# Differential attention heads turned to tokens and back by VectorE in 32 x 32 squares and DRAM, in place of TensorE transposes

## The chip, the cores and the metric

The kernel runs on one core of a Trainium2 chip, in one launch. The metric is the device time of an execution in microseconds. A core has TensorE (PE, with its weight loads PEld), VectorE (DVE), ScalarE (ACT), GpSimd (POOL) and SyncE (SP, which here issues transfers). PE writes to PSUM, in banks of 128 x 512 float32; the other tiles lie in SBUF, 128 partitions wide. Each engine works through its own queue in order; semaphores tie the queues together.

## The reference

One layer of a streaming encoder on 512 tokens of width 1024. A norm of x feeds four parallel mixers: A differential attention, B forgetting attention, C a convolution module, D a short gated convolution. Each is projected to the model width, gated, summed and projected out; then come cross-attention and a gated MLP. The change lies in mixer A, behind its attention:

```python
ya = _diff_attention(a_q..., a_k..., a_v..., lam, t_pos)      # (B, S, 4 heads, 128)
ya = (_rms_norm(ya, diff_norm[l]) * (1.0 - lambda_init)).reshape(B, S, BR_W)
...
proj = jnp.einsum('bsnc,ncd->bsnd', br, w_branch[l])          # br stacks ya, yf, yc, ys
```

For each token and head the 128 channels are divided by their root mean square, then scaled by a gain per channel.

## The kernel before, in words

**Tiling.** Activations are channel-major: channels on the partitions, the 512 tokens along the free axis. Every float32 operand is split into a high and a low part (`split`, lines 152 to 159: ACT writes the high part, DVE the low one), and each product is three matmuls (`mm3`). A block of weights of 512 KB is loaded by SP into a raw tile (`wr`, two buffers, line 176), cast by ACT to `wh` (line 190) and split by DVE to `wl` (line 191), four buffers each. `run_blocks` fetches the weights of three jobs ahead and then runs the job's body.

**A head.** `a_task(h)` does head h: in steps 0 to 3 scores of one block of 128 queries (two halves, PSUM tag `sc`), softmax on DVE and ACT, and the difference of the two (line 853); in steps 1 to 4 the probabilities of the step before are transposed on PE (tag `tr`) and split; in steps 3 and 5 `values` multiplies them with v into a bank of tag `av` (two buffers). At the end of step 5 ACT copies the bank to SBUF (line 858), channel-major, 128 channels by 512 tokens. Then the norm, lines 861 to 878: four PE transposes turn the head to tokens in a `tr` bank; ACT squares it (864), DVE sums over channels (866), POOL makes the reciprocal root (`rstd_of`, 268 and 271), DVE multiplies (868); four more PE transposes turn it back, and `split` with the gain as its scale writes `y["a"]` (tag `y8b`), which branch A's projection reads.

**What sets the order.** Three things. The jobs come in the order of `mixer_jobs`: for h = 0 to 3 the q and k projections of head h, each followed by 0, 2, 4 or 6 jobs of branch C's gate and projection; then `bg.drain("a")`, then the values of the forgetting attention (`vf_jobs`), its q and k, and between those branch A's gate and projection. The heads are background tasks (class `Background`): generators that yield a cost and a wait. A clock counts PE work (0.00042 a column of a matmul, 0.107 a transpose); at each tick, after every job and in the middle of a long one, the first two tasks of the queue may step, if credit (0.7 of the clock, at most 4) is left and the task's wait has passed. So `yield cost, 3.5` means: not again before the clock is 3.5 further. `drain` steps all tasks of a name to the end, waits or no waits. Last, the framework gives every instruction its place in the engines' queues, from this order and from its own estimate of when operands and buffers are ready.

**Buffers that matter.** In `vf_jobs` the first two token blocks take two banks of tag `mm` and two of tag `av`; the result goes to a tile of tag `v`, of which there is one, held by the heads' values (`va`) until the last head is done. Tags `ck` and `fbias` (two buffers each, 128 x 512) belong to `f_task`: rows of the cumulated log-forget and the score bias.

**A turn that is there already.** `conv_norm_task` (lines 670 to 709) turns the convolution's 512 x 512 result to tokens and back: four `V.transpose` (32 x 32 squares within a tile), four stores from SP to a DRAM tile (line 680), four loads (line 683).

Of the kernel before, what the change touches and what calls it, by code (L numbers as in the profile page):

```python
# [17 lines left out]
F32 = mybir.dt.float32  # L18
F32R = mybir.dt.float32r
AF = mybir.ActivationFunctionType  # L20
ALU = mybir.AluOpType
AX = mybir.AxisListType
# [3 lines left out]
P = 128  # L26
S = 512
# [56 lines left out]
def hybrid_layer(ctx: ExitStack, tc: tile.TileContext, a: dict, out: bass.AP):  # L84
# [12 lines left out]
    def bank(tag=None):  # L97
        if tag is None:
            turn_of.n += 1
            tag = "av" if turn_of.shared and turn_of.n % 2 else "mm"  # L100
        return psum.tile([P, 512], F32, tag=tag, name=f"ps_{tag}", bufs=2)
# [133 lines left out]
    def transpose(ps, x, n=P):  # L235
        PE.transpose(ps, x, ident[:n, :n])  # L236
        bg.clock += 0.107
# [75 lines left out]
    def e4(dtype=F32):  # L313
        return m1p.tile([P, 2, S], dtype, tag="e", name="e", bufs=3)
# [108 lines left out]
    def turn(t, half):  # L423
        ps = turned[t, half] = bank("av" if half else "tr")
        for k in range(4):
            keep(PE.transpose(ps[:, k * P:(k + 1) * P], y01[t][:, (half * 4 + k) * P:(half * 4 + k + 1) * P], ident))
# [229 lines left out]
    def conv_task(j):  # L656
# [5 lines left out]
        for k in range(n - 1):  # L662
# [4 lines left out]
                conv_ends.append(ins.ins)  # L667
            yield 0.66, 0.0

    def conv_norm_task():  # L670
        xn = m1p.tile([P, 5, S], F32, tag="qk", name="xn", bufs=2)
        tok, chan = (dram.tile([S, S], F32, name=n) for n in ("conv_tok", "conv_chan"))

        def turn(rows, squares, src):
            for i in range(4):
                V.transpose(squares[:, i], src[:, i])
                yield 0.65, 0.0
            form = rows.rearrange("(b r) (j a c) -> a r j b c", r=32, a=4, c=32)
            for a in range(4):
                SP.dma_start(form[a], squares[a * 32:a * 32 + 32].rearrange("r j (b c) -> r j b c", c=32))  # L680
            yield 0.0, 4.0
            for i in range(4):
                SP.dma_start(xn[:, i], rows[i * P:(i + 1) * P, :])
            yield 0.0, 5.0

        yield 0.0, 2.0
        while len(conv_ends) < 4:
            yield 0.0, 0.5
        yield from turn(tok, conv_u, conv_y)
        for t in range(NT):  # L690
            st = m1p.tile([P, 6], F32, tag="bn6", name="bn6", bufs=2)
            mv = m1p.tile([P, 2], F32, tag="bn2", name="bn2", bufs=2)
            V.bn_stats(st, xn[:, t])
            V.bn_aggr(mv, st)
            r = rstd_of(m1p, [mv[:, 1:2]])
            V.tensor_scalar(xn[:, t], xn[:, t], mv[:, 0:1], r, ALU.subtract, ALU.mult)
            yield 1.5, 0.0
        yield from turn(chan, conv_y, xn)
        while "d" in y:
            yield 0.0, 2.0  # L700
        yield 0.0, 2.0
        y["c"] = (y8(), y8())
        for j in range(4):
            e = e4()
            A.activation(e[:, 0], xn[:, j], AF.Identity, bias=pc("ln_b", j), scale=pc("ln_g", j))
            A.activation(e[:, 1], xn[:, j], AF.Tanh, bias=half["ln_b"][:, j:j + 1], scale=half["ln_g"][:, j:j + 1])
            V.scalar_tensor_tensor(e[:, 0], e[:, 1], 1.0, e[:, 0], ALU.add, ALU.mult)
            split(e[:, 0], y["c"][0][:, j], y["c"][1][:, j], 0.5)
            yield 1.4, 1.0
# [109 lines left out]
                m1p.tile([P, 4, 256], F32R, tag="ptl", name="ptl", bufs=2))  # L819


    def a_task(h, qk, v):
        es, pt, av = {}, None, None
        for step in range(6):
            if step in (3, 5):
                if av is None:
                    av = bank("av")
                vh, vl = (x[:, :, h * P:(h + 1) * P] for x in v[0])
                values(av, lambda kt: ((vh[:, kt], 0), (vh[:, kt], 1), (vl[:, kt], 0)), pt, step // 2 - 1)
            cost = 0.0  # L830
            if 1 <= step <= 4:
                if step in (1, 3):
                    pt = pt_tiles()
                to_keys_major(es.pop(step - 1)[:, 0], step, pt[0], pt[1], (step - 1) % 2)
                cost += 0.1 + 0.15 * step
            if step < 4:
                qt, w = step, (step + 1) * P
                e = es[qt] = e4()
                st = m1p.tile([P, 8], F32, tag="st8", name="st8", bufs=4)
                for c in range(2):  # L840
                    ps = bank("sc")
                    scores(ps, qk, c, qt * P, w)
                    V.tensor_tensor_reduce(e[:, c, :w], ps[:, :w], mask_a[:, S - w:], scale=1.0,
                                           scalar=-3.0e38, op0=ALU.add, op1=ALU.max,
                                           accum_out=st[:, c:c + 1])
                V.tensor_scalar(st[:, 2:4], st[:, 0:2], -HD ** -0.5, None, ALU.mult)
                for c in range(2):
                    A.activation(e[:, c, :w], e[:, c, :w], AF.Exp, bias=st[:, 2 + c:3 + c],
                                 scale=HD ** -0.5, accum_out=st[:, 4 + c:5 + c])
                V.reciprocal(st[:, 6:8], st[:, 4:6])  # L850
                V.tensor_scalar(st[:, 7:8], st[:, 7:8], lam, None, ALU.mult)
                A.activation(e[:, 1, :w], e[:, 1, :w], AF.Copy, scale=st[:, 7:8])
                V.scalar_tensor_tensor(e[:, 0, :w], e[:, 0, :w], st[:, 6:7], e[:, 1, :w], ALU.mult,
                                       ALU.subtract)
                cost += 0.6 + 0.0035 * w
            if step == 5:
                e = e4()
                A.copy(e[:, 0], av)
            yield cost, 3.5

        ps = bank("tr")
        for t in range(NT):
            transpose(ps[:, t * P:(t + 1) * P], e[:, 0, t * P:(t + 1) * P])
        A.activation(e[:, 1], ps, AF.Square, scale=1.0 / math.sqrt(P))
        ms = m1p.tile([P, NT], F32, tag="ms4", name="ms4", bufs=2)
        V.tensor_reduce(ms, e[:, 1].rearrange("p (t c) -> p t c", t=NT), AX.X, ALU.add)
        r = rstd_of(m1p, [ms], NT)
        V.tensor_tensor(e[:, 0].rearrange("p (t c) -> p t c", t=NT),
                        ps.rearrange("p (t c) -> p t c", t=NT),
                        r.unsqueeze(2).to_broadcast([P, NT, P]), ALU.mult)  # L870
        yield 1.5, 3.5
        ps2 = bank("tr")
        for t in range(NT):
            transpose(ps2[:, t * P:(t + 1) * P], e[:, 0, t * P:(t + 1) * P])
        if "a" not in y:
            y["a"] = (y8b(), y8b())
        split(ps2, y["a"][0][:, h], y["a"][1][:, h], half["dn"])
        yield 0.6, 0.0


# [874 lines left out]
```

## Time and profile before

| | us |
|---|---|
| median of 3 runs | 1061.96 (1061.37 to 1063.41) |
| the profiled execution | 1061.46 |
| its span, first to last instruction | 1059.7 |
| PE busy in the span | 1048.7 |

In rows of instructions the columns are start, duration, engine, line, operation, output and inputs, shapes and count; a value in brackets is the idle time ahead and what ended it. Grouped rows give the busy time (overlapping instructions counted once) and the mean ns of one. The view of one source line gives minimum, median and maximum ns, first and last start, and below it what the engine waited for ahead of these instructions, or who waited for them, as microseconds and times. Rows of waits read: who, for whom, total, times, longest. In the rows of windows stand the busy time and count of PE, PEld, DVE, ACT and POOL, PE's granted clock, the DMA share and GB/s.

### The profile page before, as it was taken

Reading aid. Unit: us, or ns where it says so; the run is one execution under the profiler, and the core shown is the slowest. Engines: PE = TensorE matmul, PEld = TensorE weight load, DVE = VectorE, ACT = ScalarE, POOL = GpSimd, SP = SyncE. Lnnn points to the kernel's source line nnn. Section 1 sums busy time; section 2 is a strip of 40 time slices with the busy share of each in tenths; the row PEclk is TensorE's granted clock in tenths of the full one; section 3 lists DMA queues with packets and bytes.
Section 4 is the critical chain, followed back from the end, with each engine's and each line's share of the span. In section 5 each row is a group of like instructions: output and inputs, shape, how many; then the busy total and the mean of one; then the engine's idle time right before and its main releaser. Section 6 shows DMA issues by size and latency. Waiting matters only on the chain.

```text
span 1059.7 us, 14546 instructions
## 1 busy us (share of the span) xinstructions
PE 1048.7 (99%) x5343; PEld 891.8 (84%) x5343; DVE 800.8 (76%) x1270; ACT 497.9 (47%) x819; POOL 150.8 (14%) x249
## 2 busy tenths in 40 slices
PE   9999999999999999999999999999999999999997
PEld 8888888878888988888888899999888888888886
DVE  6999997577666358766575888886778788777796
ACT  5322222277465255655443665654333333445672
POOL 4001000100001015322100031031111211111011
PEclk9999999999999999999999999999999999999999
DMA  8854335732222243322344734226566776725662
GB/s 269 300 153 104 104 97 128 198 113 80 80 80 68 59 135 100 97 84 80 120 140 154 268 133 120 80 81 199 179 229 211 235 230 209 236 80 179 210 216 80
DMA packets 179773, 156.78 MB, mean 148 GB/s; under 512 B 22207, under 2 KB 151852, under 8 KB 179701
## 3 DMA queue, kind: packets, MB, share of 16 engines
q1 hardware_dynamic: 170659, 124.10, 38.9%
q10 hardware_dynamic: 6482, 23.21, 5.8%
q0 software_dynamic: 2560, 8.54, 2.8%
q8 instruction: 42, 0.69, 0.3%
q14 instruction: 30, 0.25, 0.1%
HBM read 135.89 MB, written 19.94 MB: 147 GB/s over the span
## 4 chain that ended last, share of the span: by engine, by line
PE 95%; DMA 1%; DVE 1%; ACT 1%; issue 0%; POOL 0%; SPq 0%; POOLq 0%; DVEq 0%; ACTq 0%
PE ps_mm L232 51%; PE ps_av L232 29%; PE ps_sc L232 7%; PE ps_tr L232 4%; PE ps_tr L236 3%; DMA xn<-conv_tok 1%; PE ps_mm L442 1%; PE ps_av L442 1%; DMA conv_chan<-y 0%; PE ps_mm L384 0%; SPq L680 0%; PE ps_sc L389 0%; DMA xn<-conv_chan 0%; DVE wl L191 0%; POOL st_r L271 0%
## 5 line engine op out<-in xcount | busy, mean ns | idle before, releaser
L190 ACT CAST wh<-wr 128x1024 fp32r<-128x1024 f32 (+1 forms) x142 | 148.6, 1049 | 273.5 <-PE ps_mm L232 185.6
L191 DVE TENSOR_TENSOR wl<-wr,wh 128x1024 fp32r<-128x1024 f32 (+1 forms) x142 | 178.1, 1256 | 80.9 <-ACT wh L190 80.3
L232 PE MATMUL ps_mm<-hth,wh 128*128 128x512 f32 (+1 forms) x616 | 231.4, 382 | 2.4 <-DVE qk L777 1.9
L232 PE MATMUL ps_mm<-htl,wh 128*128 128x512 f32 (+1 forms) x616 | 230.1, 380 | 0.0
L232 PE MATMUL ps_mm<-hth,wl 128*128 128x512 f32 (+1 forms) x616 | 229.9, 380 | 0.0
L232 PEld LDWEIGHTS ps_mm<-hth,wh 128*128 128x128 f32 x616 | 114.1, 188 | 24.5 <-issue 2.3
L232 PEld LDWEIGHTS ps_mm<-hth,wl 128*128 128x128 f32 x616 | 114.0, 188 | 21.3
L232 PEld LDWEIGHTS ps_mm<-htl,wh 128*128 128x128 f32 x616 | 114.1, 188 | 20.3
L232 PE MATMUL ps_av<-htl,wh 128*128 128x512 f32 (+1 forms) x328 | 122.5, 373 | 0.0
L232 PE MATMUL ps_av<-hth,wh 128*128 128x512 f32 (+1 forms) x328 | 122.4, 373 | 0.0
L232 PE MATMUL ps_av<-hth,wl 128*128 128x512 f32 (+1 forms) x328 | 122.4, 373 | 0.0
L664 DVE SCALAR_TENSOR_TENSOR y<-y,par,y 128x482 f32<-128x482 f32 (+29 forms) x120 | 82.9, 727 | 0.2
L232 PEld LDWEIGHTS ps_av<-hth,wh 128*128 128x128 f32 x328 | 61.6, 188 | 10.9
L232 PEld LDWEIGHTS ps_av<-hth,wl 128*128 128x128 f32 x328 | 61.6, 188 | 10.9
L232 PEld LDWEIGHTS ps_av<-htl,wh 128*128 128x128 f32 x328 | 61.6, 188 | 10.8
L1548 DVE TENSOR_TENSOR wl<-dw,wh 128x1024 fp32r<-128x1024 f32 x32 | 40.2, 1260 | 13.2 <-ACT wh L1547 13.0
L1547 ACT CAST wh<-dw 128x1024 fp32r<-128x1024 f32 x32 | 33.4, 1051 | 23.3 <-PE ps_tr L232 8.5
L1002 POOL TENSOR_SCALAR fbias<-ck,cq 128x128 f32<-128x128 f32 (+3 forms) x32 | 27.5, 865 | 68.9 <-DVE st L1008 63.7
L1496 ACT ACTIVATE th<-c 128x512 f32<-128x512 f32 x22 | 13.9, 632 | 48.3 <-DVE c L594 48.2
L155 ACT CAST pth<-ps_tr 128x512 fp32r<-128x512 f32 (+3 forms) x56 | 23.4, 448 | 22.0 <-PE ps_tr L236 21.9
L594 DVE SCALAR_TENSOR_TENSOR c<-ps_mm,par,c 128x510 f32<-128x510 f32 (+1 forms) x44 | 32.7, 744 | 0.7
L156 DVE TENSOR_TENSOR ptl<-ps_tr,pth 128x512 fp32r<-128x512 f32 (+3 forms) x56 | 27.9, 513 | 6.1 <-ACT pth L155 5.9
(469 smaller groups left out, 2102.9 us busy)
## 6 DMA issues: line engine op xcount, KB each, us to landing
wr<-in_w_up SPq DMA_DIRECT2D x44, 512.0 KB
wr<-in_w_in SPq DMA_DIRECT2D x38, 512.0 KB
wr<-in_w_gate SPq DMA_DIRECT2D x32, 512.0 KB
wp<-in_w_down ACTq DMA_DIRECT2D x22, 512.0 KB
sums<-wp ACTq DMA_DIRECT2D x22, 512.0 KB
dw<-sums SPq DMA_DIRECT2D x44, 256.0 KB
wr<-in_w_branch SPq DMA_DIRECT2D x16, 512.0 KB
wide<-in_w_out SPq DMA_DIRECT2D x12, 512.0 KB
```

Of the source, the lines that this page charges most:

```text
L155: A.copy(hi, ps)
L156: V.tensor_tensor(lo, ps, hi.bitcast(F32), ALU.subtract)
L190: order(A.copy(hi, raw[:, :n]))
L191: low.tensor_tensor(lo, raw[:, :n], hi.bitcast(F32), ALU.subtract)
L232: PE.matmul(ps, lhs, rhs, start=start, stop=stop)
L236: PE.transpose(ps, x, ident[:n, :n])
L442: keep(PE.matmul(banks[c][:, :S // 2], w[p == 1][:, k, c * P:(c + 1) * P], ht[p == 2][:, i * 4 + k, :S // 2], start=(i, p, k) == (0, 0, 0) ...
L594: ins = V.scalar_tensor_tensor(dst[:, s:], src[:, :S - s], w(k), dst[:, s:], ALU.mult, ALU.add)
L664: ins = V.scalar_tensor_tensor(dst[:, s:], src[:, :S - s], pc("conv_dw", k * 4 + j), dst[:, s:], ALU.mult, ALU.add)
L1002: G.tensor_scalar(bias[:, :w], ck[j][:, :w], -1.0, cq[:, qt, head:head + 1], ALU.mult, ALU.add)
L1547: A.copy(hi, x)
L1548: V.tensor_tensor(lo, x, hi.bitcast(F32), ALU.subtract)
```

## The change

Two helpers are added beside `conv_norm_task`: `squares`, a VectorE transpose of 32 x 32 squares with a rearranged output, and `turn`, a generator that transposes by squares into the tile `between`, stores that to a DRAM tile of 256 KB in rows of 2 KB, and loads it into `dst` in four transfers of 32 partitions in pieces of 512 bytes. With the squares' places exchanged on the way, the tile is transposed as a whole. In `a_task` the eight PE transposes go; the bank is copied to a tile of tag `ck` in place of `e`, turned to tokens, normed in SBUF (channels now in four groups of 32), turned back, brought to token order by one more ACT pass that also applies the gain, and split from SBUF without a scale. The yields change with it: 3.5, 3.5 after the copy become 3.5, 0.5, 4.0, 5.0, 1.0, 0.5, 4.0, 5.0.

```diff
+    def squares(dst, src, n):
+        V.transpose(dst.rearrange("p (b n c) -> p n b c", b=4, c=32), src.rearrange("p (n b c) -> p n b c", b=4, c=32))
+
+    def turn(dst, src, n, between, name, blocks_first=False):
+        t = dram.tile([P, n * P], F32, name=name)
+        if blocks_first:
+            V.transpose(between, src)
+        else:
+            squares(between, src, n)
+        yield 0.1 + 0.14 * n, 0.5
+        SP.dma_start(t, between)
+        yield 0.0, 4.0
+        form = t.rearrange("(i r) (b x) -> b r i x", r=32, b=4)
+        for b in range(4):
+            SP.dma_start(dst[b * 32:b * 32 + 32].rearrange("r (i x) -> r i x", i=4), form[b])
+        yield 0.0, 5.0
...
+    def head_tile(tag):
+        return m1p.tile([P, S], F32, tag=tag, name=f"head_{tag}", bufs=2)
...
             if step == 5:
-                e = e4()
-                A.copy(e[:, 0], av)
+                o = head_tile("ck")
+                A.copy(o, av)
             yield cost, 3.5

-        ps = bank("tr")
-        for t in range(NT):
-            transpose(ps[:, t * P:(t + 1) * P], e[:, 0, t * P:(t + 1) * P])
-        A.activation(e[:, 1], ps, AF.Square, scale=1.0 / math.sqrt(P))
+        sq = head_tile("fbias")
+        x = head_tile("ck")
+        yield from turn(x, o, NT, sq, f"head_tok{h}")
+        A.activation(sq, x, AF.Square, scale=1.0 / math.sqrt(P))
         ms = m1p.tile([P, NT], F32, tag="ms4", name="ms4", bufs=2)
-        V.tensor_reduce(ms, e[:, 1].rearrange("p (t c) -> p t c", t=NT), AX.X, ALU.add)
+        V.tensor_reduce(ms, sq.rearrange("p (a t c) -> p t a c", a=4, t=NT), AX.XY, ALU.add)
         r = rstd_of(m1p, [ms], NT)
-        V.tensor_tensor(e[:, 0].rearrange("p (t c) -> p t c", t=NT),
-                        ps.rearrange("p (t c) -> p t c", t=NT),
-                        r.unsqueeze(2).to_broadcast([P, NT, P]), ALU.mult)
-        yield 1.5, 3.5
-        ps2 = bank("tr")
-        for t in range(NT):
-            transpose(ps2[:, t * P:(t + 1) * P], e[:, 0, t * P:(t + 1) * P])
+        x4 = x.rearrange("p (a t c) -> p a t c", a=4, t=NT)
+        V.tensor_tensor(x4, x4, r.unsqueeze(1).unsqueeze(3).to_broadcast([P, 4, NT, 32]), ALU.mult)
+        yield 1.5, 1.0
+        o = head_tile("ck")
+        sq = head_tile("fbias")
+        yield from turn(o, x, NT, sq, f"head_chan{h}", True)
         if "a" not in y:
             y["a"] = (y8b(), y8b())
-        split(ps2, y["a"][0][:, h], y["a"][1][:, h], half["dn"])
+        z = head_tile("fbias")
+        A.activation(z.rearrange("p (t b c) -> p t b c", t=NT, b=4), o.rearrange("p (b t c) -> p t b c", b=4, t=NT),
+                     AF.Identity, scale=half["dn"])
+        split(z, y["a"][0][:, h], y["a"][1][:, h])
         yield 0.6, 0.0
```

## The prediction

> **What bounds the kernel now.** I read first the busy shares and the chain that ended last, then what TensorE (PE) waited for, then the stretch in which the four heads run.
>
> ```profile
> span 1059.7 us, 14546 instructions
> PE 1048.7 (99%) x5343; PEld 891.8 (84%) x5343; DVE 800.8 (76%) x1270; ACT 497.9 (47%) x819; POOL 150.8 (14%) x249
> PE 95%; DMA 1%; DVE 1%; ACT 1%; issue 0%; POOL 0%; SPq 0%; POOLq 0%; DVEq 0%; ACTq 0%
> PE ps_mm L232 <- DVE qk L777: 1.9, 1, 1.9
> 258.00:360.00 102.00, 102.00 (x571) 88.52 (x570) 63.56 (x144) 53.03 (x107) 8.93 (x15) 1.00 0.25 73
> ```
>
> The chain is 95% PE. From 258 to 360 us, where the heads are normed, PE is busy all 102 us at granted clock 1.00, VectorE (DVE) 63.56, ScalarE (ACT) 53.03. The only PE wait of note, 1.9 us, lies ahead of that stretch. So what is taken out of PE's queue here shortens the kernel one for one, as long as nothing new makes PE wait.
>
> **What is removed.** Eight transposes a head, 32 in all.
>
> ```profile
> L236 PE MATMUL ps_tr<-ident,e 128*128 128x128 f32 x152 | 23.2, 273 | 0.0
> 276.32 0.39 PE L232 MATMUL ps_mm<-htl,wh 128*128 128x512 f32 x1
> 276.55 0.39 PE L232 MATMUL ps_mm<-hth,wl 128*128 128x512 f32 x1
> 276.78 0.60 PE L236 MATMUL ps_tr<-ident,e 128*128 128x128 f32 x4
> 277.13 0.48 PE L232 MATMUL ps_mm<-hth,wh 128*128 128x512 f32 x1
> 277.45 0.40 PE L232 MATMUL ps_mm<-htl,wh 128*128 128x512 f32 x1
> ```
>
> One transpose lasts 273 ns, but they overlap. Matmuls start 0.23 us apart (276.32, 276.55). Without the four transposes the next two would have started at 276.78 and 277.01; the second started at 277.45. So four cost 0.44 us, one 0.11. Eight such groups: **3.5 us**, the lower bound; the upper one is by busy time, 23.2 / 152 x 32 = 4.9 us. I take 3.5, since starts are what pace PE.
>
> [...]
>
> **What is added, off PE.**
>
> ```profile
> L676 DVE STREAM_TRANSPOSE y<-xn x4: 671/680/705, 195.1 to 199.2; 128x512 f32<-128x512 f32 x4
> L866 DVE TENSOR_REDUCE ms<-e x4: 675/679/685, 271.1 to 353.9; 128x4 f32<-128x512 f32 x4
> L868 DVE TENSOR_TENSOR e<-ps_tr,st_r x4: 672/684/692, 274.4 to 356.0; 128x512 f32<-128x512 f32 x4
> L159 DVE SCALAR_TENSOR_TENSOR y8b<-ps_tr,s_dn,y8b x4: 751/752/752, 280.4 to 360.5; 128x512 fp32r<-128x512 f32 x4
> L156 DVE TENSOR_TENSOR y<-e,y x4: 680/694/695, 428.6 to 527.6; 128x512 fp32r<-128x512 f32 x4
> L158 ACT ACTIVATE y<-e x4: 620/624/633, 216.8 to 222.9; 128x512 fp32r<-128x512 f32 x4
> ```
>
> DVE gets two transposes a head (0.68 each, by L676) and its last subtract is 0.69 in place of 0.75; reduce and multiply keep their size. That is 1.3 us a head, 5.2 in all, into 38 us of idle DVE (102 less 63.56). ACT gets one more pass of 0.62 a head, 2.5 in all, into 49 idle us. The scattered output of the first transpose has no row; between the contiguous 0.68 and three times that, the four cost at most 5.4 us more, and DVE has the room, so I take 0.68. All of this costs nothing while PE is fed; with the cover gone, a head's additions are about 2 us.
>
> Each head is turned twice, and each turn is one 256 KB store and four 64 KB loads from SP: 40 issues.
>
> ```profile
> ck<-crows POOLq DMA_DIRECT2D x8, 256.0 KB, 4.0
> crows<-e POOLq DMA_DIRECT2D x1, 16.0 KB, 2.1
> L683 SPq DMA_DIRECT2D xn<-conv_chan x4: 345/428/432, 208.5 to 209.9; - x4
> SPq L176 <- DVE wl L191: 84.5, 12, 17.0
> L232 PE MATMUL ps_mm<-y8b,wh x64: 388/389/500, 408.6 to 507.9; 128*128 128x512 f32 x64
> ```
>
> 40 issues at 0.43 us are 17 us of SP; in 255 to 375 us SP sat 84.5 us waiting for DVE to free a raw weight buffer. Behind a head's store, which waits for DVE, and behind its loads, which wait for the store, stand the weight loads (L176), and ACT's casts wait for those. The nearest rows say 2.1 to 4.0 us for the store and 4.0 for the loads; with issues and transpose a turn is 8 to 11 us, a head's tail 19 to 25 with the arithmetic between. Its reader is branch A's projection, whose first matmul is at 408.6; head 3 is copied out of PSUM at 349.76, so it would be ready near 375. That is hidden by more than 30 us.
>
> **What moves: the planner.** Tasks carry due times, and only two of the queue run at once. A tail had two waits of 3.5 in the planner's clock; now it has 3.5, 0.5, 4, 5, 1, 0.5, 4, 5, which is 23.5 against 7. Counting that clock along the code (0.215 per 512-wide matmul; positions, not times): before, head 0 ended at 232, heads 2 and 3 began at 236 and 264, and the drain came at 303, with only head 3's last half tail left. After: 253, 256, 278 and 298. Head 3's step 3 is then issued behind the last gate block of branch C, and its steps 4 and 5 and both tails fall into the drain, just ahead of the values of the forgetting attention (vf). Those need the PSUM bank that head 3 holds until its copy, and the SBUF tile of head values until its last product. This is the place that decides.
>
> ```profile
> 330.61 1.09 PE L232 MATMUL ps_sc<-qk 128*128 128x512 f32 x4
> 337.45 0.75 DVE L853 SCALAR_TENSOR_TENSOR e<-e,st 128x512 f32<-128x512 f32 x1
> 342.78 0.60 PE L236 MATMUL ps_tr<-ident,e 128*128 128x128 f32 x4
> 344.31 0.68 DVE L156 TENSOR_TENSOR ptl<-ps_tr,pth 128x512 fp32r<-128x512 f32 x1
> 346.92 0.39 PE L232 MATMUL ps_mm<-y,wl 128*128 128x512 f32 x1
> 347.63 0.28 PE L232 MATMUL ps_av<-pth,v 128*128 128x256 f32 x1
> 349.76 0.59 ACT L858 COPY e<-ps_av 128x512 f32<-128x512 f32 x1 [1.58 <-PE ps_av L232]
> 351.05 0.28 PE L232 MATMUL ps_mm<-wh,hth 128*128 128x256 f32 x1
> 351.17 0.28 PE L232 MATMUL ps_mm<-wl,hth 128*128 128x256 f32 x1
> ```
>
> Before, head 3's scores ran at 330.61, 16 us ahead of the end of the last gate block (346.92). After, they run about at its end. From then the chain is 7.6 us to the probabilities (330.61 to 338.20), 2.2 through transpose and split (342.78 to 344.99), 2.1 of values (347.63 to 349.76), 0.6 of copy: 12.5 us. PE's work meanwhile: vf's first half is 96 matmuls at 0.12 us (351.05, 351.17), 11.5 us, of which the quarter in head 3's bank must wait, so 8.6; with head 3's own scores, transposes and values, some 4.5 more: 13.1. The two match within a microsecond. Head 2's tail now stands in the same ACT and DVE queues, up to 4.6 us of it (DVE 4 x 0.68, ACT 3 x 0.62); so PE stalls between 0 and about 5 us. I take **1 us**, since ACT and DVE work side by side and little of the tail must precede the chain.
>
> **Sum.** The profiled run took 1061.46 us (span 1059.7, 1.76 around it), 0.5 under the median 1061.96. 1061.46 - 3.5 + 1.0 = 1058.96; I say **1059.0**, its own range 1056.6 (4.9 gained, no stall) to 1060.0.
>
> **Rivals.**
>
> 1. The stall at the drain is larger. The chain and the head-2 operations run one behind the other: 4 to 5 us of stall, -3.5 + 4.5 gives 1062.5, or with 3 us 1061, no change. For it: two heads' tails meet there, and nothing else can run on PE, as vf holds all four banks of its kind. Against: before the change PE never waited there.
>
> 2. The transfers hold up ACT and DVE in order, and PE behind them: **slower**. The conv norm already turns a tile in this way, twice, and the 1.9 us PE stall follows from it:
>
> ```profile
> 185.35 5.85 DMA xn<-conv_tok
> 203.44 4.95 DMA conv_chan<-y
> 208.91 2.81 DMA xn<-conv_chan
> 220.14 0.68 DVE qk L777
> 223.02 2.08 PE ps_mm L232 x8
>   ACT e L705: 2.0, 1
> ```
>
> The chain runs through both turns into the DVE work that q and k wait for, and PE resumes at 223.02; the last row is ACT's wait for the second turn's loads, 2.0 us. If each head's two turns cost as much, 4 x 1.9 = 7.6 us, less 3.5: 1065.6. It decides once ACT's square or its scaling pass stands at the head of its queue 2 us before its load lands, as in that row, with a cast that PE needs behind it. Against: 256 KB against 1 MB a turn, and these heads have no q or k standing right behind them.
> [...]
>
> 3. The 3.5 us are hidden anyway, because the weights set the pace: then 1061.5. Against, in the heads' stretch ACT's casts wait for PE far more than for loads:
>
> ```profile
>   PE ps_mm L232: 11.5, 7
>   DMA wr<-in_w_in: 1.4, 2
> ```
>
> 4. The change doesn't do what it says, the order of PE's other work shifting at random by more than the transposes: either sign, a few microseconds.
>
> **How the numbers follow.** Forecast 0.45; rival 1 0.22; rival 2 0.23; rival 3 0.04; rival 4 0.06. About 0.2% (2.1 us) is what a measurement of this kernel can tell from no change; its runs span 1061.37 to 1063.41. Faster than 1059.84: 0.42 of the forecast, 0.03 of rival 4, so 0.45. Within 0.2%: 0.03 of the forecast, 0.14 of rival 1, 0.01 of 2, rival 3, so 0.22. Slower: 0.08 of rival 1, 0.22 of 2, 0.03 of 4, so 0.33. The range reaches from 1057.0 to rival 2's 1066.0.
>
> **What would show it.** 32 fewer transposes of L236 (ps_tr from e), and PE matmul starts in the heads' stretch closed up by 0.44 us a group. A PE wait near 340 to 360 on ACT's copy of ps_av or on the cast into v is the stall at the drain, right at 0 to 2 us. ACT or DVE idle time put down to the loads of head_tok and head_chan, and PE waits on pth, qk or bank releases after it, would be rival 2. Branch A's first projection matmul must not wait for y8b. I would be wrong if PE waits in 258 to 400 us add up to over 2 us.

## The result, and the profile after

| | before | after |
|---|---|---|
| median, six runs each on the same chip | 1062.32 (1061.37 to 1063.41) | 1065.99 (1065.01 to 1067.70) |
| the profiled execution | 1061.46 | 1066.00 |
| its span | 1059.7 | 1064.2 |
| mean granted clock in it | 0.998 | 0.995 |

The ratio is 1.0036, 95% interval 1.0024 to 1.0047: the kernel became 3.8 us slower where 3 us of gain were forecast. (Below, a ratio is always to the kernel before, run beside it on the same chip, the bracket behind it is its 95% interval, and a figure in us is the ratio's distance from 1, or that between two ratios, times 1062.)

From the page of the kernel after, the span, the busy row and the chain by engine:

```profile
span 1064.2 us, 14558 instructions
PE 1048.9 (99%) x5311; PEld 890.8 (84%) x5311; DVE 804.7 (76%) x1278; ACT 501.0 (47%) x823; POOL 155.5 (15%) x249
PE 91%; DMA 3%; DVE 2%; ACT 1%; issue 1%; SPq 1%; POOL 1%; POOLq 0%; DVEq 0%; ACTq 0%
```

PE runs 32 matmuls less (5311 for 5343), yet it is busy as long as before (1048.9 for 1048.7), and its share of the chain falls from 95% to 91%, while that of transfers rises from 1% to 3%. The transposes did go, as the row of that group shows (152 of them and 23.2 us before):

```profile
L236 PE MATMUL ps_tr<-ident,e 128*128 128x128 f32 x120 | 18.4, 273 | 0.0
```

Two things took their place. The first is waits of PE; before, the view of waits from 230 to 400 us had none. After (who, for whom, total, times, longest):

```profile
PE ps_mm L232 <- DVE v L156: 1.6, 1, 1.6
PE ps_mm L232 <- DVE qk L796: 1.1, 1, 1.1
PE ps_av L232 <- ACT pth L155: 0.7, 1, 0.7
PE ps_av L232 <- ACT head_ck L880: 0.7, 1, 0.7
PE ps_av L232 <- DVE ptl L156: 0.3, 1, 0.3
PE ps_mm L232 <- DVE qk L805: 0.2, 1, 0.2
```

They are 4.6 us. The second is the clock. Three windows of the kernel after, then two of the kernel before (busy time and count of PE, PEld, DVE, ACT, POOL, then PE's clock):

```profile
222.00:228.00 6.00, 5.40 (x17) 4.32 (x18) 3.66 (x5) 3.39 (x6) 0.05 (x1) 0.72 0.49 134
258.00:360.00 102.00, 100.09 (x531) 86.06 (x530) 66.19 (x149) 53.77 (x107) 7.29 (x13) 0.98 0.35 104
354.00:360.00 6.00, 4.79 (x25) 4.45 (x26) 3.04 (x7) 1.56 (x5) 0.00 (x0) 0.73 0.24 88
```

```profile
222.00:228.00 6.00, 4.98 (x22) 4.16 (x23) 4.05 (x6) 3.81 (x6) 0.48 (x1) 1.00 0.52 147
354.00:360.00 6.00, 6.00 (x53) 6.00 (x52) 2.52 (x6) 1.33 (x4) 1.21 (x2) 1.00 0.01 1
```

Twice the clock fell to 0.72 or 0.73 over six microseconds. PE's rows show what that is: the 512-wide matmuls, 0.23 us apart at 223.37, start 0.43 apart from 223.99 on, until 226.98.

```profile
223.37 0.40 PE L232 MATMUL ps_mm<-hth,wh 128*128 128x512 f32 x1
223.60 0.60 PE L232 MATMUL ps_mm<-htl,wh 128*128 128x512 f32 x1
223.99 0.63 PE L232 MATMUL ps_mm<-hth,wl 128*128 128x512 f32 x1
224.42 0.63 PE L232 MATMUL ps_mm<-hth,wh 128*128 128x512 f32 x1
...
226.98 0.43 PE L232 MATMUL ps_mm<-hth,wh 128*128 128x512 f32 x1
```

A clock of 0.72 over 6 us loses 6 x 0.28 = 1.7 us, one of 0.73 loses 1.6. So the balance of the two profiles is -3.5 (transposes, at the forecast's price) + 4.6 (waits) + 3.3 (clock) = +4.4; the spans differ by 4.5.

The waits lie in two places. Those on pth, ptl and head_ck lie at the drain, where head 3 meets the values of the forgetting attention (vf). PE's rows there, with the wait and its cause in brackets:

```profile
342.51 0.86 PE L232 MATMUL ps_sc<-qk 128*128 128x512 f32 x3
343.73 0.45 PE L232 MATMUL ps_sc<-qk 128*128 128x512 f32 x1
354.20 0.38 PE L232 MATMUL ps_av<-pth,v 128*128 128x256 f32 x1 [0.67 <-ACT pth L155]
354.92 0.39 PE L232 MATMUL ps_av<-ptl,v 128*128 128x256 f32 x1 [0.34 <-DVE ptl L156]
357.09 0.59 PE L232 MATMUL ps_av<-wh,hth 128*128 128x264 f32 x1 [0.67 <-ACT head_ck L880]
```

Head 3's last scores moved from 330.61 to 342.51, and vf waits for its bank until 357.09. Those on v and qk come later, at 374 and 387 us. ACT's rows ahead of them, and from the chain the head's transfers (start, duration to landing):

```profile
372.06 1.05 ACT L190 CAST wh<-wr 128x1024 fp32r<-128x1024 f32 x1 [3.03 <-DMA wr<-in_w_in]
373.01 0.37 ACT L155 CAST v<-ps_mm 128x256 fp32r<-128x256 f32 x1
...
379.92 0.72 ACT L899 ACTIVATE head_fbias<-head_ck,s_dn 128x512 f32<-128x512 f32 x1 [2.33 <-DMA head_ck<-head_chan]
380.66 1.28 ACT L962 ACT_TABLE_LOAD   x1
```

```profile
370.59 5.95 DMA head_chan<-head_fbias
377.92 1.93 DMA head_ck<-head_chan
```

The scaling pass of head 3 (L899) stood 2.33 us at the head of ACT's queue for these transfers; the logarithm of the forget gates (L962, for which a table is loaded first), the cast of the next weights and the casts of q and k stand behind it. The wait on v is of another kind: ahead of the casts of v ACT stood 3.03 us for a block of weights. That block was hardly late, for without the transfers (third experiment) the same cast starts at 371.63; but there, as before the change, two of the four casts of v stand ahead of it in ACT's queue, and here none.

### The profile page after: what moved, and what is told of

The parts are those of the page before. It is cut to its first block, busy times and chain, and to the rows that moved or that the text cites. A ratio compares the mean times of both kernels' runs of the same rounds, so it can differ in the third digit from the quotient of the medians.

```text
span 1064.2 us, 14558 instructions
## 1 busy us (share of the span) xinstructions
PE 1048.9 (99%) x5311; PEld 890.8 (84%) x5311; DVE 804.7 (76%) x1278; ACT 501.0 (47%) x823; POOL 155.5 (15%) x249
## 4 chain that ended last, share of the span: by engine, by line
PE 91%; DMA 3%; DVE 2%; ACT 1%; issue 1%; SPq 1%; POOL 1%; POOLq 0%; DVEq 0%; ACTq 0%
PE ps_mm L232 48%; PE ps_av L232 29%; PE ps_sc L232 7%; PE ps_tr L232 4%; PE ps_tr L236 3%; DMA head_chan<-head_fbias 1%; PE ps_mm L442 1%; PE ps_av L442 1%; DVE wl L191 0%; DMA xn<-conv_tok 0%; DMA conv_chan<-y 0%; ACT wh L190 0%; DMA head_ck<-head_chan 0%; SPq L699 0%; DMA xs<-in_x 0%
```

## The experiments

Four causes had to be told apart: the planner's longer waits, which move the heads (theory 1); instructions that stand in order in front of loads that have not landed (theory 2); a clock that falls after a short wait or not, by chance (theory 3); and the gain itself, 3.5 us or less (theory 4).

### A square of kernels: waits and transfers, each with and without

**Transfers kept, waits as before.** (The cost of 0.66 that each turn counts goes with its waits.)

```diff
-        yield 0.1 + 0.14 * n, 0.5
+        yield 0.0, 0.0
...
-        yield 0.0, 4.0
+        yield 0.0, 0.0
...
-        yield 0.0, 5.0
+        yield 0.0, 0.0
...
-        yield 1.5, 1.0
+        yield 1.5, 3.5
```

> The changed kernel with the planner's waits as they were before the change: the turn's three waits are 0, the norm's is 3.5; the turns and their transfers stay. Theory 1 (the long waits push the tails of heads 2 and 3 and head 3's last steps into the drain): head 3's scores run some 10 us before the end of the last gate block again, the PE waits on pth, ptl and head_ck at 354 to 357 us (1.7 us) and the half-clock stretch behind them (1.3 us) go; what is left is the gain of 3.5 us less the waits for the transfers (2.7 us): the ratio to the kernel before is 0.998 to 1.000, about 1061.5 us. Theory 2 (ACT and DVE stand in order behind the transfers): nothing of the 2.7 us ahead of v and qk goes, it may grow as the tail has no slack left: 1064 us or more, ratio 1.002 to 1.005. [...]

Measured: 1063.14, ratio 1.0012 (1.0003 to 1.0021). The drain stall went, as theory 1 has it, and the rest stayed, as theory 2 has it; the total lies between the two. Rows of ACT in this kernel's profile, then of PE:

```profile
305.27 0.72 ACT L899 ACTIVATE head_fbias<-head_ck,s_dn 128x512 f32<-128x512 f32 x1 [2.99 <-DMA head_ck<-head_chan]
305.90 0.71 ACT L870 ACTIVATE e<-e,st 128x512 f32<-128x512 f32 x1
...
310.11 0.58 ACT L804 CAST qk<-ps_mm 64x512 fp32r<-64x512 f32 x1
```

```profile
312.76 0.33 PE L232 MATMUL ps_sc<-qk 128*128 128x128 f32 x1 [0.82 <-ACT qk L804]
313.58 0.30 PE L232 MATMUL ps_sc<-qk 128*128 128x128 f32 x1 [0.49 <-DVE qk L805]
```

One head's scaling pass waits 2.99 us for its load; another head's softmax and its q and k stand behind it, and PE then waits 0.8 and 0.5 us for them. At the drain head 3's square stood 8.10 us for its load, with casts of v behind it, for which PE waited 1.2 us. The clock from 312 to 318 us was 0.74, 1.6 us more. The store that this load waited for had been issued 0.6 us behind a weight load of 512 KB and took 4.66 us to land.

**Waits as after, PE transposes as before.**

```diff
+        yield 0.66, 0.5
+        yield 0.0, 4.0
+        yield 0.0, 5.0
         ps = bank("tr")
...
-        yield 1.5, 3.5
+        yield 1.5, 1.0
+        yield 0.66, 0.5
+        yield 0.0, 4.0
+        yield 0.0, 5.0
         ps2 = bank("tr")
```

> The kernel before, with its PE transposes and without any turn or transfer, but with the waits of the changed kernel in the planner (0.5, 4, 5 ahead of the first four transposes, 1 after the multiply, 0.5, 4, 5 ahead of the second four). Theory 1: head 3's scores move to the end of the last gate block, PE waits about 1.7 us for pth, ptl or the copy of ps_av there, with up to 1.3 us of half clock behind it: 1064 to 1065.5 us, ratio 1.0015 to 1.003, though nothing is turned through DRAM. Theory 2: no waits ahead of v at 374 and qk at 387 us, and no drain stall either, as ACT's square waits for no load: ratio 0.999 to 1.001.

Measured: 1064.85, ratio 1.0025 (1.0015 to 1.0035), with no turn through DRAM at all. PE's rows at the drain:

```profile
357.21 0.38 PE L232 MATMUL ps_av<-pth,v 128*128 128x256 f32 x1 [0.24 <-ACT pth L155]
357.93 0.39 PE L232 MATMUL ps_av<-ptl,v 128*128 128x256 f32 x1 [0.34 <-DVE ptl L156]
360.09 0.66 PE L236 MATMUL ps_tr<-ident,e 128*128 128x128 f32 x4 [0.68 <-ACT e L858]
```

The stall is the same one, 1.3 us of it. Theory 1 is shown, at 2.7 us.

**Waits as after, no transfers.**

```diff
-        SP.dma_start(t, between)
...
-        for b in range(4):
-            SP.dma_start(dst[b * 32:b * 32 + 32].rearrange("r (i x) -> r i x", i=4), form[b])
+        G.tensor_copy(dst, between)
```

> The changed kernel, its waits in the planner kept, with the store and the four loads of each head's turn replaced by one GpSimd copy from the turn's squares to its target; the exchange of the squares' places is left out, so the norm is taken over a mixed set of values. Theory 1: the PE waits at the drain (1.7 us) and the half clock behind them stay, the others go: 1061.5 to 1063.5 us, ratio 0.999 to 1.001. Theory 2: the waits ahead of v (1.6 us) and qk (1.1 us) go, and with them most of what the drain lost, as ACT's square no longer waits 1.7 us inside it: 1059 to 1061 us, ratio 0.997 to 0.999.

Measured: 1060.68, ratio 0.9988 (0.9979 to 0.9997). At the drain the waits are what they were (0.7, 0.7 and 0.3 us, and a clock of 0.72 from 354 to 360 us); that on v is gone and that on q and k fell to 0.3. So ACT's wait inside the drain (1.66 us for the load of head 2) was not what made that stall, against what theory 2 had claimed of it.

**Neither.** The two edits above together: the copy by GpSimd, and the waits 0, 0, 0 and 3.5.

> The changed kernel with both suspects taken away: each turn's store and loads are one GpSimd copy (the exchange of the squares' places is left out, so the norm is taken over a mixed set of values), and the planner's waits are those of before. What is left of the change is 32 transposes less on PE and the added work of DVE, ACT and POOL. If the loss is the sum of a planner part and a transfer part (after 1.0036, transfers alone 1.0012, planner waits alone 1.0025, neither turn nor transposes 0.9974): 1059.0 to 1060.0 us, ratio 0.997 to 0.9985, no drain stall, no wait ahead of qk above 0.5 us other than the 1.9 at 222 us. If the added DVE and ACT work itself costs: 1061 us or more, ratio above 0.9992.

Measured: 1058.21, ratio 0.9964 (0.9950 to 0.9977), a little below the range expected: the added work of DVE and ACT costs nothing that the intervals could tell, and the gain is 3.8 us. In its profile PE is busy 1045.2 us, 3.5 less than before.

**No turn and no transposes**, in the kernel before (`e[:, 0]` stands for the banks in what follows):

```diff
-        ps = bank("tr")
-        for t in range(NT):
-            transpose(ps[:, t * P:(t + 1) * P], e[:, 0, t * P:(t + 1) * P])
-        A.activation(e[:, 1], ps, AF.Square, scale=1.0 / math.sqrt(P))
+        A.activation(e[:, 1], e[:, 0], AF.Square, scale=1.0 / math.sqrt(P))
...
-        split(ps2, y["a"][0][:, h], y["a"][1][:, h], half["dn"])
+        split(e[:, 0], y["a"][0][:, h], y["a"][1][:, h], half["dn"])
```

> The kernel before with the eight transposes a head left out and nothing in their place: the norm is taken channel-major over the wrong axis, from SBUF; the planner's waits are those of before. It measures the most that the change could gain. The forecast's price (32 transposes at 0.11 us of PE starts) gives 3.5 us: 1058.8 us, ratio 0.9967 (0.9955 to 0.998 with what the order of the rest may shift). By busy time, 4.9 us: 1057.4, ratio 0.9954. If the transposes were hidden, no change: 0.999 to 1.001.

Measured: 1059.37, ratio 0.9974 (0.9964 to 0.9985), 2.8 us. Forecast 3.5 lies in the interval of both this and the last kernel.

The square, as ratios:

| | waits of before | waits of after | difference |
|---|---|---|---|
| no transfers | 0.9964 | 0.9988 | 2.5 us |
| transfers through SP | 1.0012 | 1.0036 | 2.5 us |
| PE transposes | 1 | 1.0025 | 2.7 us |
| difference of the first two rows | 5.1 us | 5.1 us | |

The parts add up: -3.8 + 2.5 + 5.1 = +3.8 us, which is what the change cost. By the intervals of the ratios each difference is uncertain by an estimated 1.1 to 1.7 us; both parts are larger than that.

### What in the transfers costs

**The tails apart.** Turns and norm of a head run as a task of their own, one at a time, outside the queue's two places and the drain:

```diff
-        sq = head_tile("fbias")
-        x = head_tile("ck")
-        yield from turn(x, o, NT, sq, f"head_tok{h}")
+        bg.tails.append([a_tail(h, o), 0.0])
+
+    def a_tail(h, o):
+        sq = head_tile("fbias")
+        x = yield from turn(None, o, NT, sq, f"head_tok{h}")
...
-        yield 0.0, 5.0
+        yield 0.0, 7.0
```

> The changed kernel with each head's turns and norm as a background task of its own: it takes none of the two places of the queue, the drain ahead of the values of the forgetting attention does not step it, one tail runs at a time, and the wait after the loads is 7 in place of 5; all is computed. Theory 1 and 2 together (the loss is the tails' time in the queue and the drain, and ACT standing in front of loads that have not landed): the drain stall goes, the ACT waits shrink below 1 us each: 1059.5 to 1061 us, ratio 0.9975 to 0.999. Rival (the transfers cost wherever they stand, through the ring of SP that the weights share): ratio 1.001 or more, with PE waits behind ACT's casts of weights that landed late.

Measured: 1061.60, ratio 0.9996 (0.9987 to 1.0005), between the two ranges that were expected. The drain stall went, but ACT still waited 9.9 us in four times for the second loads, once (1.7 us) at 379.93 among the casts of q and k, and PE 1.6 us behind it.

**Readers on GpSimd**, once in the tail apart, once in the first experiment's kernel (in both the scale of the square moves to a small pass of DVE, and in the tail apart 1.5 of wait stand behind the square):

```diff
-        A.activation(sq, x, AF.Square, scale=1.0 / math.sqrt(P))
+        G.tensor_tensor(sq, x, x, ALU.mult)
...
-        A.activation(z.rearrange("p (t b c) -> p t b c", t=NT, b=4), o.rearrange("p (b t c) -> p t b c", b=4, t=NT),
-                     AF.Identity, scale=half["dn"])
-        split(z, y["a"][0][:, h], y["a"][1][:, h])
+        G.tensor_scalar(z.rearrange("p (t b c) -> p t b c", t=NT, b=4), o.rearrange("p (b t c) -> p t b c", b=4, t=NT),
+                        half["dn"], None, ALU.mult)
+        G.tensor_copy(y["a"][0][:, h], z)
+        G.tensor_tensor(y["a"][1][:, h], z, y["a"][0][:, h], ALU.subtract)
```

> As the tail apart, and the readers of the loads moved off ACT and DVE: GpSimd squares the tokens, scales the head by the gain and writes its high and low part; DVE keeps the sum over channels, the multiply and the squares. All is computed. If ACT in front of a load is what makes PE wait: no ACT wait on head_ck is left, 1059 to 1060.5 us, ratio 0.997 to 0.9985, at or below the tail apart. If the SP ring is what costs: no better than the tail apart. If GpSimd is too slow and DVE now stands behind it: DVE waits on POOL and PE waits on DVE, ratio above 1.001.

> The first experiment (planner waits as before, turns and transfers kept, tails in the head's task), with the readers of the loads on GpSimd in place of ACT as above. It changes only which engine stands in front of the loads. That experiment gave 1.0012 against 0.9974 with no turn at all, 4.0 us. Theory 2 (ACT in order): the ACT waits on head_ck of 9.1 and 4.3 us go and with them the PE waits ahead of scores and values (1.3 and 1.2 us) and the half-clock stretch at 312 us (1.5 us): 1060 to 1061 us, ratio 0.998 to 0.9995. Rival (ring of SP, late weights, or DVE now waiting for GpSimd): ratio 1.001 or more.

Measured: 1062.98, 1.0009 (0.9997 to 1.0020), and 1062.29, 0.9997 (0.9988 to 1.0006). In the tail apart the wait only changed place: DVE stood 6.5 us in front of GpSimd's squares, and PE waited 2.5 us for DVE's forget gates. In the other, 1.6 of the 5.1 us came back, though no instruction of ACT waits for a head's load any more. Its groups of GpSimd and DVE show where the waiting went (busy, mean ns, then idle time ahead and its cause):

```profile
L900 POOL TENSOR_SCALAR head_fbias<-head_ck,s_dn 128x512 f32<-128x512 f32 x4 | 7.2, 1801 | 29.9 <-DMA head_ck<-head_chan 29.9
L892 DVE TENSOR_TENSOR head_ck<-head_ck,st_r 128x512 f32<-128x512 f32 x4 | 2.8, 689 | 2.0 <-POOL st_r L271 2.0
```

**Transfers issued by GpSimd**: with ACT's readers, with GpSimd's readers (both with the waits of before), and with the tail apart and GpSimd's readers.

```diff
-        SP.dma_start(t, between)
+        G.dma_start(t, between)
...
-            SP.dma_start(dst[b * 32:b * 32 + 32].rearrange("r (i x) -> r i x", i=4), form[b])
+            G.dma_start(dst[b * 32:b * 32 + 32].rearrange("r (i x) -> r i x", i=4), form[b])
```

> The first experiment (planner waits as before) with one thing changed: the stores and loads of the heads' turns are issued by GpSimd in place of SP, so that they stand in another queue than the weights; all is computed. If the queue shared with the weights is what costs (a store took 4.66 us to land behind a weight load, and weights come late behind the head's loads): 1059.5 to 1061.5 us, ratio 0.998 to 1.000, against 1.0012 through SP. If it is ACT standing in front of loads that have not landed, whichever queue they come by: no better, 1.001 to 1.003, as GpSimd's issues are slower.

> The readers on GpSimd (planner waits as before; ratio 0.9997 with SP's queue) and the turns' transfers issued by GpSimd too; all is computed. What was left there was the wait of 2.2 us ahead of qk at 382 us, behind a weight load that took 5.3 us to land after four loads of the head in the same queue, and 1.6 us of half clock behind it. If that queue is the cause: the weight load lands within 3 us of its issue, the wait ahead of qk falls below 0.7 us: 1058.5 to 1060 us, ratio 0.9965 to 0.998. If it is the DMA engines and not the queue: no change, 0.999 to 1.001.

> The tail as a task of its own with its readers on GpSimd (ratio 1.0009), and its transfers issued by GpSimd too, with 1 more of wait behind the squares; all is computed. There DVE's part of the forget gates stood behind the tail (PE waited 2.5 us for it). If the SP queue was behind that: 1059 to 1061 us, 0.997 to 0.999. If it is where the tail of head 3 falls (beside the forget gates and the q and k of the next mixer, 370 to 388 us): no better than 1.0005.

Measured: 1061.12, 0.9990 (0.9981 to 0.9999); 1061.42, 0.9991 (0.9982 to 1.0001); 1061.54, 0.9994 (0.9985 to 1.0004). The first recovers 2.3 us. Its issues of transfers (KB each, median us to landing):

```profile
head_tok<-head_fbias POOLq DMA_DIRECT2D x4, 256.0 KB, 2.3
head_ck<-head_tok POOLq DMA_DIRECT2D x16, 64.0 KB, 2.2
```

A store lands in 2.3 us here, against 3.85 and 4.66 for the two stores that stand in the chain of the first experiment's kernel, which go through SP, and ACT's waits for the loads fall from 13.4 to 6.2 us. One issue takes GpSimd longer than SP, as was expected (0.58 us by L972 of the kernel before, against 0.43 by L686 of the first experiment's kernel). What the second queue saved is probably that the store no longer lay behind 512 KB of weights; that is an estimate from these landing times, which no run tells apart. The second kernel of the three was expected to add the gains of both edits and did not: PE still waited 1.3 us for its q and k, and the weight load ahead of them still took 5.75 us to land. The head's transfers are not what makes that load slow, though: the load in the same place of the chain took 5.01 us in the kernel with neither. The third kernel fell between its two ranges. All three lose 1.8 us at the end of the kernel, which is shown below.

**GpSimd's readers without transfers** (the readers' edit on the kernel with neither):

> The kernel without transfers and with the planner's waits of before (a GpSimd copy in place of each turn's store and loads, so the norm is over a mixed set; ratio 0.9964), with the readers of the turned tiles on GpSimd as in the experiments that gave 0.9997 and 0.9991. Between 0.9991 and 0.9964 lie 2.9 us that are not yet told. If they are the price of GpSimd as reader (1.0 to 1.8 us a pass): ratio 0.9985 to 0.9995 here. If they belong to the transfers: 0.996 to 0.9975 here.

Measured: 1057.56, 0.9957 (0.9943 to 0.9971). As readers, GpSimd's passes, up to 1.8 us each, cost nothing; the transfers cost 4.2 us with these readers through SP (0.9997) and 3.6 through GpSimd (0.9991).

**Transfers that nobody waits for**, in the kernel without transfers:

```diff
         G.tensor_copy(dst, between)
+        t, t2 = (dram.tile([P, n * P], F32, name=name + c) for c in "ab")
+        SP.dma_start(t, between)
+        form = t.rearrange("(i r) (b x) -> b r i x", r=32, b=4)
+        for b in range(4):
+            SP.dma_start(t2[b * 32:b * 32 + 32].rearrange("r (i x) -> r i x", i=4), form[b])
...
+        sq = head_tile("fbias")
         A.activation(sq, x, AF.Square, scale=1.0 / math.sqrt(P))
```

The square gets a tile of its own here, as the stored one must not change under the store. In the second kernel GpSimd issues the same transfers; its store takes a constant tile (`mask_a`) and is placed behind the copy.

> The same kernel without transfers (ratio 0.9964, ACT and DVE as readers), and each turn's store and four loads issued by SP all the same, at their old places, the loads from the stored tile to a second DRAM tile that nobody reads. So no instruction of ACT or DVE waits for them; SP's queue and the DMA engines carry them in full. The transfers cost 5.1 us in all (1.0012 less 0.9964). If that is ACT standing in front of the loads: 0.9960 to 0.9975 here. If it is the weights held up behind them in SP's queue or on the DMA engines: 0.9985 to 1.001, with ACT's casts waiting for weights at 366 to 376 us. Both in parts: in between, and the ratio says how much.

> The same with the idle transfers issued by GpSimd (the store takes a tile that is never changed). SP's queue then carries weights alone, the DMA engines the same bytes. If what the weights lose is the place in SP's queue: 0.996 to 0.997 here against more through SP. If it is the DMA engines' time: the same as through SP within 0.0008.

Measured: 1058.85, 0.9967 (0.9956 to 0.9977) through SP, and 1060.28, 0.9981 (0.9970 to 0.9991) through GpSimd. The first run tells traffic from waiting: all 40 transfers in SP's queue among the weights, all their bytes on the DMA engines, and the time is that of the kernel without them (0.9964) within its interval. PE's waits from 200 to 430 us are down to the one at 222 us:

```profile
PE ps_mm L232 <- DVE qk L797: 1.9, 1, 1.9
```

So the bytes and the 40 issues cost nothing as they stand there; it takes an instruction that waits. That the weights in SP's queue never come late is not shown by it, for its last idle load is issued by 361.1 us and the next weight load at 364.68. In the kernel with GpSimd's readers and SP's queue (0.9997), where no instruction of ACT waits for a head's load, the loads of head 3 stand right ahead of that weight load:

```profile
364.65 1.73 SPq L686 DMA_DIRECT2D head_ck<-head_chan  x4
366.48 1.02 SPq L176 DMA_DIRECT2D wr<-in_w_in  x2
371.87 1.05 ACT L190 CAST wh<-wr 128x1024 fp32r<-128x1024 f32 x1 [3.57 <-DMA wr<-in_w_in]
```

With neither transfers nor longer waits it was issued at 364.50 and cast at 368.21. The chain runs on from this cast through DVE to q and k, for which PE waits 2.16 us at 382.91, and the clock from 376 to 388 us was 0.86, another 1.7. So there the transfers cost through a late weight.

That GpSimd's queue came out worse with idle transfers, which neither expectation had, does not lie with the heads: branch A's first projection starts at 406.2 us there, and at 406.5 in the kernel without transfers. It lies at the end. The last pass of DVE in the kernel without transfers (span 1057.3), then in this one (span 1058.4):

```profile
1052.91 1.54 DVE L1665 SCALAR_TENSOR_TENSOR o<-o,st_r,res 128x512 f32<-128x512 f32 x3 [0.71 <-POOL st_r L271]
1052.08 1.54 DVE L1671 SCALAR_TENSOR_TENSOR o<-o,st_r,res 128x512 f32<-128x512 f32 x3 [0.71 <-POOL st_r L271]
```

It is 0.8 us ahead at this pass and 1.1 us behind at the end. From the start of this pass to the end of the span go 6.2 to 6.3 us in all five kernels whose turns GpSimd issues, and 4.4 to 4.5 in the other 13. These 1.8 us come behind all computing; what fills them the profiles don't show. In the first kernel with GpSimd's queue (0.9990) branch A's projection starts at 406.4 us, as early as without transfers. So an estimated 2.3 + 1.8 = 4.1 of the 5.1 us came back there, with ACT still the reader: by this estimate most of what the transfers cost it is how late they land through SP.

**Waits at the loads.** The transfers stay; the norm's 3.5 goes, and 3.5 stands behind each turn's loads. A tail then waits 10.5 in all, where the first experiment and the kernel before have 7. The edit against the first experiment:

```diff
             SP.dma_start(dst[b * 32:b * 32 + 32].rearrange("r (i x) -> r i x", i=4), form[b])
-        yield 0.0, 0.0
+        yield 0.0, 3.5
...
-        yield 1.5, 3.5
+        yield 1.5, 0.0
```

> The first experiment (transfers through SP, planner waits as before, ratio 1.0012) with the tail's waits moved and their sum kept: the norm's 3.5 goes, and 3.5 stands after each turn's loads, where the reader would else come too early (10.5 in all with the 3.5 behind the copy, where that experiment and the kernel before have 7, and the changed kernel 23.5). All is computed. If the transfers cost only through readers that come before their loads: ACT's waits on head_ck (9.1 and 4.3 us) fall below 5 in all, 1060 to 1062 us, ratio 0.998 to 1.0002. If the longer sum pushes the tails into the drain again: a drain stall, ratio 1.001 or more.

> The same move of the waits, with the transfers issued by GpSimd (ratio 0.9990 before the move, with ACT waits on head_ck of 4.2 and 2.0 us). If readers that come too early are the cause: below 0.9985, about 1059.5 us, the best of the kernels that compute all. If the waits only shift the stall to the drain: 0.999 or more.

Measured: 1060.30, 0.9989 (0.9979 to 0.9998), and 1060.45, 0.9989 (0.9979 to 0.9999). Through SP this recovers 2.4 us, by two numbers in the code. PE's waits there, 1.9 us of the first row being the one at 222 us:

```profile
PE ps_mm L232 <- DVE qk L796: 2.3, 2, 1.9
PE ps_mm L232 <- DVE v L156: 0.9, 1, 0.9
PE ps_sc L232 <- DVE qk L805: 0.4, 1, 0.4
```

One part of what was expected missed: ACT's waits for the loads did not fall below 5 us, they are 12.2. But 7.8 of these are one wait at the drain, ahead of head 3's square, where PE has vf to do and lost 0.9 us (the row on v); what fell is the waits with q and k behind them (the scaling pass 2.0 us, from 4.3). With GpSimd's queue the move adds nothing that the intervals could tell. As the sum of the waits grew too, place and length are not told apart. Both kernels compute all and are faster than the kernel before, by 0.01% to 0.21%: a small gain, but the change's 3.8 us of loss are gone.

## Why the prediction was wrong, point by point

- **The removed transposes: right.** Taken 3.5 us by the starts; the two kernels that keep only the removal gave 2.8 and 3.8. The 4.9 by busy time lies above both values, but inside the interval of the second (2.4 to 5.3).
- **DVE's and ACT's added passes at nothing: right.** The kernel with neither the longer waits nor transfers, but with all the added passes, is no slower than the one without any turn (0.9964, 0.9974). The transpose with scattered output, for which no row stood before, took 0.71 us in the kernel after, beside 0.69 of the contiguous one.
- **The 40 issues and the turns' latency at nothing: this step failed, by 5.1 us.** The prediction said that the tail "would be ready near 375" for a reader at 408.6, "hidden by more than 30 us". That reader did not wait, as forecast: head 3's tail ended at 383.5, and its projection begins at 413.4. But the latency was priced for the tail's last reader alone. Its first readers are the square and the scaling pass on ACT, and ACT works in order: a wait of theirs for a load (2.99 us at 305.27 in the first experiment, 2.33 at 379.92 in the kernel after) was a wait for the softmax, the cast of weights and the q and k behind it. How much of the 5.1 us goes this way is not measured apart. With the readers on GpSimd only 1.6 us came back, and in that kernel a weight came late behind the head's loads (cast at 371.87), which the prediction had named and priced at nothing too; with no reader at all the transfers cost nothing (0.9967 against 0.9964).
- **The stall at the drain at 1 us: right in kind and place, too small.** The waits of the planner cost 2.5 to 2.7 us in three pairs of kernels. In the profile head 3's chain took 14.5 us from its first score (342.51) to the end of its copy (357.04) where 12.5 were added up, against 13.1 of cover: a stall of 1.7 us, and the half clock behind it added 1.6 there.
- **The rivals: both came, and the sum had 1 us for the first and nothing for the second.** They were set up as cases that exclude each other, with 4.5 and 7.6 us; each came at about 60% of its price (2.5 and 5.1), and together they outweighed 3.8 of gain. The place that rival 2 named as its condition, "ACT's square or its scaling pass stands at the head of its queue 2 us before its load lands, ... with a cast that PE needs behind it", is the row at 379.92 (2.33 us). What the prediction held against it, that no q or k stand right behind these heads, was wrong: each head is followed by the next head's q and k, and the last by vf's gates.
- **The bound that would show it wrong**, PE waits of more than 2 us from 258 to 400 us, was passed: 4.6.

What stays open: between the best kernels with transfers (0.9989) and the one without (0.9964) lie 2.7 us. Through SP the profile shows 1.7 of them as PE waits; through GpSimd 1.8 lie at the end of the kernel, and whether that end can be avoided was not tried.

## What to carry to other kernels

Price the latency of a transfer at its first reader and not at its last: look what stands in that reader's queue behind it, and whether PE needs it; and look what stands behind the transfer in its own queue. Where a planner issues by due times, a short wait behind the load paid here (10.5 in all, 2.4 us gained); a much longer sum (23.5) moves the whole task, and the stall reappears at the next place where tasks are forced to end. And two rivals that rest on different mechanisms can both come: their expected prices belong in the sum and not only in the chances.

## What the runs showed of the hardware

Behind a wait of 1.9 us PE ran at half clock for 3.4 us in half of the profiles (in the kernel after from 223.60 to 226.98, its matmuls 0.43 us apart in place of 0.23) and not in the other half; nothing that they show decides which, and so it is called chance here. All 18 profiles of this study (before, after and 16 experiments) have a wait for q and k that ends between 222 and 225 us, 1.73 to 1.88 us long, ahead of all that was edited. In nine of them the clock from 222 to 230 us was 0.79, in the other nine 1.00. The clock of one kernel differs from run to run as well: over the 21 runs of the kernel before that stand beside the last two experiments, its mean over the span goes from 0.996 to 0.999. This is one such pair, the kernel with the idle transfers through SP and through GpSimd:

```profile
222.00:230.00 8.00, 7.21 (x25) 5.80 (x26) 3.84 (x5) 3.65 (x7) 0.24 (x1) 0.79 0.39 106
```

```profile
222.00:230.00 8.00, 6.17 (x30) 5.05 (x29) 5.11 (x8) 5.23 (x9) 1.04 (x2) 1.00 0.47 131
```

A clock of 0.79 over 8 us is 1.7 us (3.4 us at half), so of two waits of nearly the same length (1.88 and 1.83 us) the first cost 3.6 us with the clock behind it, and the second no more than itself; and of the 4.5 us between the two profiles shown first, 1.7 are this chance and not the change. Theory 3 is shown in that.
